# Layer 0 by quarters of the modulation, and later modulation units moved behind queries and values

## The chip, the cores and the metric

The kernel runs on one core of a Trainium2 chip, one launch for the whole model. The metric is the device time of one execution, in microseconds (us); lower is better. TensorE multiplies, VectorE (DVE) and ScalarE (ACT) do elementwise work, GpSimd (POOL) does little here but issue some DMAs, and SyncE (SP) issues nearly all the loads.

## The reference, cut to what matters

The model has two parts of two layers each, on 256 tokens of 1024 features. The change lies in the first part, whose layer is:

```python
c_act = jax.nn.silu(c)
for l in range(DEPTH):                               # DEPTH = 2
    mod = c_act @ w_ada[l] + b_ada[l]                # a vector times 1024 x 6144
    sh1, sc1, g1, sh2, sc2, g2 = jnp.split(mod, 6, axis=-1)
    h = modulate(rmsnorm(x, norm_mix_g[l]), sh1, sc1)   # h * (1 + sc1) + sh1
    proj = h @ w_in[l]                               # conv a, conv gate, q, k, v: 5 x 512 columns
    ...
    y_conv = conformer_conv(u_conv, ...)
    y_att = chunk_band_attention(q, k, v, ..., rel_bias[l])   # 8 heads of 64
    x = x + g1 * (concatenate([y_conv, y_att], -1) @ w_out[l])
    h = modulate(rmsnorm(x, norm_ffn_g[l]), sh2, sc2)
    x = x + g2 * f(h)                                # layer 0 swiglu, layer 1 mixture of experts
```

The six sections of `mod` are numbered 0 to 5 below, in the order sh1, sc1, g1, sh2, sc2, g2.

## The kernel before

Products with weights run in fp32 made of three fp32r products: a 1 MB chunk of weights is loaded (tile `raw`, four buffers for all loads), ScalarE casts its high half and VectorE subtracts to get its low half (`split`, L183 to L188), and `mm3` (L190 to L193) issues high x high, high x low and low x high. A group of 512 output columns (`ca`, `cg` for the conv, `k`, `q`, `v`) is two chunks of four 128-row blocks each, for two tiles of 128 tokens: 48 matmuls of 128x512.

**Modulation.** Sections 0 and 1 of layer 0 are needed first, and are made by quarters of 256 columns (`mod_first`, L402). Of a quarter, section 0 is multiplied on TensorE (L434, the vector's eight pieces as stationary tiles of one column) and section 1 on VectorE (L426, L428). The row of section 0 is copied by ScalarE (L435, `mrow`), then both are turned into columns by tiny matmuls into `mqc` (L447, L448), and ScalarE adds the bias (L449 to L451). `norm_mod` (L455) then scales and shifts the transposed normalized x (`tr`) into the high and low halves `n10h`, `n10l`. The code makes the products of quarter q + 1 in the step of quarter q, and the projections are issued after all quarters.

All other sections are *fillers*, `mod_acc` (L289): a unit loads 1 MB of `w_ada` (two row blocks, `ada` L301) and VectorE adds each block, times its piece of the vector, to an accumulator of 128x1024 (L306, two updates per unit, four units per section). The first unit of a section clears the accumulator on POOL (L297) and loads the section's row of `b_ada` into it (L298). When a section is complete, TensorE sums over partitions, into columns (`mod_cols`, L314, tile `mc`) or rows (`mod_rows`, L326). `mix1` of layer 0 gets the 12 units of sections 2, 3 and 4, and pops one after each chunk of the five projection groups (in `grp`, L503) and one in each of the four attention pairs, with what is left in the last (L751 to L755). Section 5 and the 24 units of layer 1 go to the feed-forward part.

**Attention.** Heads go in four pairs. `bias_of` (L629) loads a pair's relative bias by two DMAs on SP (L637) into one tile and POOL fills two corners (L640, L641). VectorE adds it to the scores `s` and takes maxima (L663, `sbig`), TensorE transposes (`pt`) and multiplies with v (`po`). Convolution products (`cvp`, L617, stationary tiles of 32 columns) run between. At the end come the output projection (chunks `wo040`, `wo041`, `wo000`, `wo001`) and the residual.

A tile framework's scheduler sets the order of instructions on each engine and of the loads from the order of the code, the dependences and the free buffers, so code that stands later may come earlier on an engine that has time by its reckoning.

Of the kernel before, what the change touches and what calls it, by code (L numbers as in the profile page):

```python
# [11 lines left out]
F32 = mybir.dt.float32  # L12
# [5 lines left out]
ALU = mybir.AluOpType  # L18
# [3 lines left out]
P = 128  # L22
# [52 lines left out]
def kernel(ctx: ExitStack, tc: tile.TileContext, I: dict, out: bass.AP, dbg=None, upto=99):  # L75
# [212 lines left out]

    def mod_acc(l, sec, accp):  # L289
# [3 lines left out]
        def unit(k0):  # L293
            def f():
                if k0 == 0:
                    st["acc"] = accp.tile([P, D], F32, tag="acc", name=f"acc{l}{sec}")
                    G.memset(st["acc"], 0.0)  # L297
                    nc.sync.dma_start(st["acc"][0:1, :], I["b_ada"][l : l + 1, sec * D : (sec + 1) * D])  # L298
# [6 lines left out]
                for k in range(2):  # L305
                    V.scalar_tensor_tensor(  # L306
# [8 lines left out]
    def mod_cols(l, which, sec, acc, gain=None):  # L315
# [85 lines left out]

    def mod_first(m, accp):  # L402
# [5 lines left out]

        rows = {}

        def products(q):
            cs = slice(q * 256, (q + 1) * 256)
            raws = []
            for sec in range(2):
# [3 lines left out]
                raws.append(raw.rearrange("p (k c) -> p k c", k=KT))  # L418
            if q == 2:
                ahead["ca0k0"] = load("ca0k0", lambda r: [(  # L420
                    r.rearrange("p (k c) -> p k c", k=4),
                    I["w_in"][0, 0:512, 0:512].rearrange("(k p) c -> p k c", p=P),
                )])
            for k in range(KT):
                if k == 0:
                    V.tensor_scalar(acc[:, cs], raws[1][:, k, :], cact[:, k : k + 1], None, op0=ALU.mult)  # L426
                else:
                    V.scalar_tensor_tensor(  # L428
                        acc[:, cs], raws[1][:, k, :], cact[:, k : k + 1], acc[:, cs], op0=ALU.mult, op1=ALU.add
                    )  # L430
            row = jp.tile([P, 256], F32, tag="tmp", name=f"mrow{q}", bufs=4)
            ps = mmps(f"mq{q}")
            for k in range(KT):
                T.matmul(ps[0:1, :256], cact[:, k : k + 1], raws[0][:, k, :], start=(k == 0), stop=(k == KT - 1))  # L434
            A.copy(row[0:1], ps[0:1, :256])  # L435
            rows[q] = row

        def quarter(q):
            if q == 0:
                products(0)  # L440
            if q < 3:
                products(q + 1)
# [12 lines left out]
    def norm_mod(pool, name, Ac, Bc, before=None):  # L455
# [1556 lines left out]
```

## Time and profile before

| | us |
|---|---|
| median of 3 runs | 2274.03 (2272.07 to 2275.12) |
| the profiled execution | 2275.15 |
| its span | 2273.4 |
| TensorE busy, share of the span | 2199.0, 97% |
| VectorE busy | 1778.3, 78% |
| mean granted TensorE clock, share of 2.4 GHz | .989 |

The times and rows below come from the profiled execution; its time is the span plus 1.7 us around it. A group's busy time adds instructions that overlap at their ends, so the distance between two starts tells what one costs. "Idle before" is the time in which the engine had nothing, and behind the arrow stands what ended it. PEclk is the clock granted to TensorE, as a share of 2.4 GHz, over a stretch, and the lower level is 1.2 GHz.

### The profile page before, as it was taken

To read this page: it belongs to the slowest core of one execution; us is meant where nothing else is said; L and a number is where in the kernel's file an instruction comes from. 1 tells how busy PE (TensorE), PEld (TensorE's weight loads), DVE (VectorE), ACT (ScalarE), POOL (GpSimd) and SP (SyncE) were. 2 spreads that over 40 slices of the span, in tenths; PEclk is the share of its full clock that TensorE was granted. 3 is DMA by queue.
4 is the path that set the end of the run, shared out by engine and by line. 5 is a ranking of instruction groups with operands and counts; after the bars stand their busy time and mean duration, and the time that the engine had idled before them with its cause. 6 is when DMAs were issued, how large, how long until landed. Compare 5 with 4: busy or idle time off the path is not lost. (4 is left out here: it accounts for less than half of the span.)

```text
span 2273.4 us, 29353 instructions
## 1 busy us (share of the span) xinstructions
PE 2199.0 (97%) x10708; PEld 1715.6 (75%) x10708; DVE 1778.3 (78%) x2878; ACT 1411.0 (62%) x2171; POOL 63.1 (3%) x173
## 2 busy tenths in 40 slices
PE   7998998998999999999999999999999999999998
PEld 4766887867878777777778777777777778777776
DVE  7778887657998888889888888987766667766676
ACT  4355334557777777777777777676565556565654
POOL 2300000200000000000000000000000000000000
PEclk9999999999999999999999999999999999999999
DMA  9968796735999999999999999997445445444442
GB/s 328 299 207 279 276 325 226 235 88 200 380 328 352 342 337 359 344 339 332 367 340 350 339 340 361 336 367 227 153 138 177 130 134 171 167 141 131 166 133 85
DMA packets 275758, 587.15 MB, mean 258 GB/s; under 512 B 22796, under 2 KB 42380, under 8 KB 275606
## 3 DMA queue, kind: packets, MB, share of 16 engines
q1 hardware_dynamic: 273302, 580.46, 73.1%
q0 software_dynamic: 2304, 4.74, 0.8%
q8 instruction: 86, 1.41, 0.3%
q14 instruction: 66, 0.54, 0.1%
HBM read 579.80 MB, written 1.05 MB: 255 GB/s over the span
## 5 line engine op out<-in xcount | busy, mean ns | idle before, releaser
L306 DVE SCALAR_TENSOR_TENSOR acc<-ada,cact,acc 128x1024 f32<-128x1024 f32 x80 | 102.3, 1280 | 2.6 <-DMA ada<-in_w_ada_dram 1.5
L491 ACT CAST at<-t 128x512 fp32r<-128x512 f32 x56 | 32.9, 587 | 87.3 <-PE t L1145 87.3
L492 DVE TENSOR_TENSOR at<-t,at 128x512 fp32r<-128x512 f32 x56 | 38.3, 684 | 22.9 <-ACT at L491 22.7
L363 ACT ACTIVATE sqj<-x 128x512 bf16<-128x512 f32 x36 | 22.6, 627 | 45.0 <-DVE x L487 28.4
L1379 ACT ACTIVATE ec<-ec,nmc 128x128 f32<-128x128 f32 x64 | 28.6, 447 | 16.8 <-DVE nmc L1375 16.8
L530 POOL DMA_DIRECT2D zst<-zp x64 | 33.8, 534 | 71.1 <-ACT zp L546 56.8
L617 PE MATMUL cvp<-zst,cw 128*32 128x256 f32 x512 | 33.5, 405 | 0.0
L1731 POOL MEMSET kbd<- 128x64 f32 x2 | 0.3, 152 | 1081.7 <-PE sc L1194 1021.7
L1105 ACT ACTIVATE gh<-g,mcol,mcol 128x256 f32<-128x256 f32 x32 | 18.3, 570 | 18.1 <-PE g L1095 18.1
L617 PEld LDWEIGHTS cvp<-zst,cw 128*32 128x32 f32 x512 | 16.9, 115 | 15.3 <-issue 5.3
L434 PE MATMUL mq<-ada,cact 128*1 128x256 f32 x64 | 17.8, 441 | 10.7 <-DMA ada<-in_w_ada_dram 10.7
L1095 PEld LDWEIGHTS g<-pm,xnt 128*128 128x128 f32 x128 | 20.5, 207 | 4.3 <-issue 2.0
L1095 PE MATMUL g<-pm,xnt 128*128 128x256 f32 x128 | 21.3, 299 | 1.9 <-DVE pm L1087 1.9
L434 PEld LDWEIGHTS mq<-ada,cact 128*1 128x1 f32 x64 | 5.7, 94 | 21.4 <-ACT sqj L363 9.5
L1375 DVE CUSTOM_DVE_ANT_0 ec<-sc,causal 128x128 f32<-128x128 f32 x64 | 19.7, 351 | 2.0 <-PE sc L1390 2.0
L1375 DVE CUSTOM_DVE_ANT_0 ea<-sa,causal 128x128 f32<-128x128 f32 (+1 forms) x32 | 10.2, 353 | 13.9 <-PE sa L1390 13.9
L667 ACT ACTIVATE sbig<-sbig,nm 128x128 f32<-128x128 f32 (+1 forms) x32 | 14.2, 446 | 10.0 <-DVE nm L663 10.0
L1196 DVE TENSOR_TENSOR yacc<-yacc,sc 128x512 f32<-128x512 f32 x28 | 17.9, 682 | 1.1 <-PE sc L1194 0.7
L1379 ACT ACTIVATE eb<-eb,nmb 128x128 f32<-128x128 f32 (+1 forms) x32 | 14.3, 447 | 6.9 <-DVE nmb L1375 6.9
L1106 ACT ACTIVATE xg<-g,mcol,mcol 128x256 fp32r<-128x256 f32 x32 | 18.3, 572 | 0.0
L1403 DVE TENSOR_SCALAR ec<-ec,smc 128x128 f32<-128x128 f32 x64 | 17.2, 316 | 0.6
L486 DVE TENSOR_TENSOR rtmp<-fd,mrow 128x512 f32<-128x512 f32 x12 | 8.1, 687 | 10.9 <-PE fd L193 10.7
(4846 smaller groups left out, 8267.5 us busy)
## 6 DMA issues: line engine op xcount, KB each, us to landing
ada<-in_w_ada_dram SPq DMA_DIRECT2D x48, 1024.0 KB, 6.8
zst<-zp POOLq DMA_DIRECT2D x64, 65.8 KB, 5.9
bias<-in_rel_bias_dram SPq DMA_DIRECT2D x8, 256.0 KB, 5.1
x<-in_x_dram SPq DMA_DIRECT2D x1, 1024.0 KB, 5.2
ca0k0r<-in_w_in_dram SPq DMA_DIRECT2D x1, 1024.0 KB
ca0k4r<-in_w_in_dram SPq DMA_DIRECT2D x1, 1024.0 KB
cg0k0r<-in_w_in_dram SPq DMA_DIRECT2D x1, 1024.0 KB
cg0k4r<-in_w_in_dram SPq DMA_DIRECT2D x1, 1024.0 KB, 5.3
```

The lines of the kernel that those rows point to most:

```text
L306: V.scalar_tensor_tensor(acc, raw[:, k * D : (k + 1) * D], cact[:, k0 + k : k0 + k + 1], acc, op0=ALU.mult, op1=ALU.add)
L363: squares["last"] = A.activation(junk, x[:, t, c * 512 : (c + 1) * 512], AF.Square, accum_out=squares["ss"][:, t, c : c + 1])
L434: T.matmul(ps[0:1, :256], cact[:, k : k + 1], raws[0][:, k, :], start=(k == 0), stop=(k == KT - 1))
L491: A.copy(dst[0][sl], ps)
L492: V.tensor_tensor(dst[1][sl], ps, dst[0][sl].bitcast(F32), op=ALU.subtract)
L530: nc.gpsimd.dma_start(z4[32 * t : 32 * (t + 1), g], zp[32 * g : 32 * (g + 1), i : i + 2, TQ * t : TQ * t + SW])
L617: T.matmul(ps[32 * g : 32 * (g + 1), :S], ws[j // (TQ // 2)][:, g, j % (TQ // 2), :], zst[i][:, g, j : j + S], start=(j == 0), stop=(j == ...
L1095: T.matmul(gp[:, i * S : (i + 1) * S], xn[part][:, t, (k + i) * P : (k + i + 1) * P], pm[:, t].rearrange("p a b -> p (a b)"), start=(n == ...
L1105: A.activation(h[:, i, :], gp[:, i * S : (i + 1) * S], AF.Identity, scale=a_, bias=b_)
L1106: A.activation(xg[0][:, k + i, :], gp[:, i * S : (i + 1) * S], AF.Identity, scale=a_, bias=b_)
L1375: V.tensor_tensor_reduce(out=e[:, SL[t]], in0=ps[:, SL[t]], in1=mask[:, SL[t]], scale=-1.0, scalar=3e38, op0=ALU.add, op1=ALU.min, accum_o ...
L1379: A.activation(e[:, SL[t]], e[:, SL[t]], AF.Exp, bias=nm[:, t : t + 1], scale=-1.0, accum_out=sm[:, t : t + 1])
```

## The change

1. `b_ada` is loaded once and transposed by TensorE into columns (`ball`). Column sections add it when they are finished (one more small VectorE operation); row sections (2 and 5) start their accumulator with a diagonal of it, by one VectorE operation. POOL's clearing and the loads of rows go, and other sections' first update is a plain multiplication.
2. Section 0's product uses a stationary tile of 32 columns (`c32`, one column filled) in four column groups, into a tile of `atps`; ScalarE copies all 128 partitions. The product of a quarter stands directly ahead of its use; the loads of the next quarter stand ahead of it.
3. In layer 0, the weights of ca, cg and k are loaded by quarters of their rows (`first_weights`: `w0a` of 2 x 128 rows for ca and cg, `w0k` of 4 x 128 rows for k), and after each quarter of the norm 36 matmuls use it (`rows_first`).
4. In layer 0, no filler is popped in the projections; three are popped per attention pair.
5. `rel_bias` is loaded from POOL's queue, in both layers.

```diff
+    ball = const.tile([P, 96], F32, name="ball")
+    brow = jp.tile([P, P], F32, tag="tmp", name="brow", bufs=4)
+    nc.sync.dma_start(brow[:96, :], I["b_ada"].rearrange("l (k p) -> (l k) p", p=P))
...
     def mod_acc(l, sec, accp):
...
-                    G.memset(st["acc"], 0.0)
-                    nc.sync.dma_start(st["acc"][0:1, :], I["b_ada"][l : l + 1, sec * D : (sec + 1) * D])
+                    if sec in (2, 5):
+                        V.tensor_tensor(
...
                 for k in range(2):
+                    if k0 + k == 0 and sec not in (2, 5):
+                        V.tensor_scalar(acc, raw[:, 0:D], cact[:, 0:1], None, op0=ALU.mult)
+                        continue
                     V.scalar_tensor_tensor(
...
+            V.scalar_tensor_tensor(r, ps[:, :KT], 1.0, bcols(l, sec), op0=ALU.add, op1=ALU.add)
+            V.tensor_tensor(r, r, gain, op=ALU.mult)
...
     def mod_first(m, accp):
...
+        c32 = accp.tile([P, D], F32, tag="acc", name="c32")[:, : KT * 32].rearrange("p (k c) -> p k c", c=32)
+        G.memset(c32, 0.0)
+        V.tensor_copy(c32[:, :, 0], cact)
...
+        def products(q):
+            cs = slice(q * 256, (q + 1) * 256)
+            ps = atps(f"mq{q}")
+            for k in range(KT):
+                g = k % 4
+                T.matmul(ps[32 * g : 32 * (g + 1), :256], c32[:, k, :], raws[q][0][:, k, :], start=(k < 4), stop=(k >= 4))
...
         def quarter(q):
             if q == 0:
-                products(0)
+                loads_of(0)
             if q < 3:
-                products(q + 1)
+                loads_of(q + 1)
+            products(q)
...
+            if after is not None:
+                after(k // 2, hT)
...
+        def rows_first(q, hT):
...
+            wa = chunk(f"w0a{q}", None, 2048)
+            if q % 2 == 0:
+                ps0["w"] = chunk(f"w0k{q}", None, 2048)
...
+            names = ("ca", "cg", "k")
+            for nm, k in [(nm, k) for k in range(2) for nm in names] if q < 3 else [(nm, k) for nm in names for k in range(2)]:
+                one(nm, k)
...
-                if fillers:
+                if fillers and not before:
                     fillers.pop(0)()
...
-                nc.sync.dma_start(
+                nc.gpsimd.dma_start(
                     bias[:, :, o : o + w], bass.AP(tensor=rb.tensor, offset=base + off, ap=[[1, P], [384, 2], [1, w]])
...
-            if fillers:
-                fillers.pop(0)()
+            for _ in range(3 if before else 1):
+                if fillers:
+                    fillers.pop(0)()
```

The order of the instructions, by engine. **SP's queue**, after the first two quarters' loads. Before (`ada0sq` is quarter q of section s, `ada0s2` and so on the filler units, a name's last number counts up through the program):

```order
L160 DMA ca0k0r_271<-in_w_in_dram 128x4x512
L417 DMA ada003_314<-in_w_ada_dram 128x8x256
L417 DMA ada013_316<-in_w_ada_dram 128x8x256
L298 DMA acc02_421<-in_b_ada_dram 1x1024
L301 DMA ada020_424<-in_w_ada_dram 128x2x1024
L160 DMA ca0k4r_428<-in_w_in_dram 128x4x512
L301 DMA ada022_460<-in_w_ada_dram 128x2x1024
L160 DMA cg0k0r_466<-in_w_in_dram 128x4x512
L301 DMA ada024_498<-in_w_ada_dram 128x2x1024
L160 DMA cg0k4r_502<-in_w_in_dram 128x4x512
L301 DMA ada026_555<-in_w_ada_dram 128x2x1024
```

and after, from the loads of the last quarter:

```order
L458 DMA ada003_408<-in_w_ada_dram 128x8x256
L458 DMA ada013_410<-in_w_ada_dram 128x8x256
L160 DMA w0a3r_412<-in_w_in_dram 128x2x1024
L160 DMA q0k0r_661<-in_w_in_dram 128x4x512
L160 DMA q0k4r_693<-in_w_in_dram 128x4x512
L160 DMA v0k0r_757<-in_w_in_dram 128x4x512
L160 DMA v0k4r_789<-in_w_in_dram 128x4x512
L318 DMA ada020_987<-in_w_ada_dram 128x2x1024
L951 DMA wr_3210<-in_moe_w_router_dram 128x8x8
L953 DMA br_3212<-in_moe_b_router_dram 1x8
L318 DMA ada022_991<-in_w_ada_dram 128x2x1024
L318 DMA ada024_995<-in_w_ada_dram 128x2x1024
```

The weights of all projections now stand ahead of every filler's load, where the two alternated.

**VectorE** ahead of the scores, from the last steps of the root (`rsqk`) to the second half of qT. Before:

```order
L145 SCALAR_TENSOR_TENSOR rsqk0y_784<-rsqk0u_783,rsqk0y_784 128x32
L143 TENSOR_TENSOR rsqk0u_783<-rsqk0y_784 128x32
L144 SCALAR_TENSOR_TENSOR rsqk0u_783<-rsqk0u_783,rsqk0v_781 128x32
L145 SCALAR_TENSOR_TENSOR rsqk0y_784<-rsqk0u_783,rsqk0y_784 128x32
L576 TENSOR_TENSOR k0_674<-k0_674,rsqk0y_784 128x512 x2
L576 TENSOR_TENSOR q0_757<-q0_757,rsqk0y_784 128x512 x2
L306 SCALAR_TENSOR_TENSOR acc04_836<-ada040_839,cact_140,acc04_836 128x1024 x2
L592 TENSOR_SCALAR qT0_882<-tr_889,vec_79 128x4x128
L306 SCALAR_TENSOR_TENSOR acc04_836<-ada042_877,cact_140,acc04_836 128x1024
L592 TENSOR_SCALAR qT0_882<-tr_901,vec_79 128x4x128
```

and after:

```order
L143 TENSOR_TENSOR rsqk0u_736<-rsqk0y_737 128x32
L326 SCALAR_TENSOR_TENSOR acc03_1096<-ada032_1101,cact_146,acc03_1096 128x1024
L144 SCALAR_TENSOR_TENSOR rsqk0u_736<-rsqk0u_736,rsqk0v_734 128x32
L326 SCALAR_TENSOR_TENSOR acc03_1096<-ada032_1101,cact_146,acc03_1096 128x1024
L145 SCALAR_TENSOR_TENSOR rsqk0y_737<-rsqk0u_736,rsqk0y_737 128x32
L326 SCALAR_TENSOR_TENSOR acc03_1096<-ada034_1191,cact_146,acc03_1096 128x1024
L655 TENSOR_TENSOR k0_650<-k0_650,rsqk0y_737 128x512 x2
L655 TENSOR_TENSOR q0_725<-q0_725,rsqk0y_737 128x512 x2
L326 SCALAR_TENSOR_TENSOR acc03_1096<-ada034_1191,cact_146,acc03_1096 128x1024
L671 TENSOR_SCALAR qT0_824<-tr_831,vec_79 128x4x128
L326 SCALAR_TENSOR_TENSOR acc03_1096<-ada036_1195,cact_146,acc03_1096 128x1024
L671 TENSOR_SCALAR qT0_824<-tr_843,vec_79 128x4x128
```

Updates of section 3 (`acc03`) stand where those of section 4 (`acc04`) stood, and more of them between the steps of the root and the scaling of k and q.

**TensorE** at the end of the pairs, about pair 2's output (`po02`), the transposed convolution (`cvT`) and the first output products (`wo`). Before:

```order
L681 MATMUL pt020_1234<-ident_83,sbig0_907 128x128 x3
L681 MATMUL pt021_1240<-ident_83,sbig0_907 128x128 x3
L730 MATMUL cvT00_1256<-ident_83,cv0_1003 128x128 x4
L730 MATMUL cvT01_1265<-ident_83,cv0_1003 128x128 x4
L191 MATMUL wo000_1316<-wo040h_1320,yT00_381 128x512
L192 MATMUL wo000_1316<-wo040l_1321,yT00_381 128x512
L193 MATMUL wo000_1316<-wo040h_1320,yT01_382 128x512
```

and after:

```order
L809 MATMUL cvT01_1270<-ident_83,cv0_945 128x128 x2
L191 MATMUL wo000_1321<-wo040h_1325,yT00_586 128x512
L768 MATMUL po02_1227<-pT020_1219,v0_754 64x256
L768 MATMUL po02_1227<-pT021_1225,v0_754 64x256
L770 MATMUL po02_1227<-pT020_1219,v0_754 64x128
L770 MATMUL po02_1227<-pT021_1225,v0_754 64x128
L191 MATMUL wo001_1322<-wo040h_1325,yT00_586 128x512
L191 MATMUL wo010_1381<-wo041h_1385,yT00_586 128x512
L338 MATMUL mc04_1246<-ones_88,acc04_1210 128x1 x8
L760 MATMUL pt030_1302<-ident_83,sbig0_849 128x128 x3
L191 MATMUL wo011_1382<-wo041h_1385,yT00_586 128x512
L760 MATMUL pt031_1308<-ident_83,sbig0_849 128x128 x3
```

The columns of section 4 (`mc04`) stood ahead of pair 1's transposes, and stand now behind the first three output products, ahead of pair 3's transposes and of the other output products.

## Rows read from the trace of the kernel before

**Rows 1.** Busy us of PE, PEld, DVE, ACT, POOL, PEclk, DMA share, GB/s

```profile
37.60:79.60 42.00, 40.11 (x168) 30.83 (x168) 32.00 (x32) 20.91 (x38) 7.31 (x13) 0.96 0.91 316
91.50:110.00 18.50, 15.58 (x66) 11.89 (x66) 13.30 (x28) 5.56 (x7) 4.76 (x9) 0.91 1.01 319
113.40:145.10 31.70, 28.45 (x347) 16.81 (x347) 22.40 (x59) 21.74 (x60) 2.15 (x7) 0.95 0.92 266
145.10:171.90 26.80, 26.80 (x129) 20.53 (x127) 22.21 (x54) 10.25 (x22) 0.00 (x0) 1.00 0.38 125
...
180.30:360.00 179.70, 178.13 (x806) 142.91 (x807) 152.84 (x154) 75.38 (x94) 4.80 (x5) 0.99 0.87 310
```

**Rows 2.** TensorE's timeline, 22 to 32 us: start, us, instruction [idle before <-releaser]

```profile
22.75 3.61 PE L434 MATMUL mq<-ada,cact 128*1 128x256 f32 x16 [0.59 <-DMA ada<-in_w_ada_dram]
30.90 1.06 PE L283 MATMUL tr<-ident,n10xn 128*128 128x128 f32 x4 [2.72 <-DVE n10h L479]
```

**Rows 3.** ScalarE's timeline, 28 to 33 us

```profile
28.52 0.56 ACT L475 ACTIVATE n10h<-tr,mcol,mcol 128x256 fp32r<-128x256 f32 x1
...
30.14 2.01 ACT L185 CAST ca0k0h<-ca0k0r 128x1024 fp32r<-128x1024 f32 x2
```

**Rows 4.** TensorE's timeline, starts of 128x512 matmuls at two times

```profile
40.05 0.39 PE L192 MATMUL ca0p<-ca0k0l,n10h 128*128 128x512 f32 x1
40.28 0.39 PE L193 MATMUL ca0p<-ca0k0h,n10l 128*128 128x512 f32 x1
...
48.50 0.63 PE L191 MATMUL ca0p<-ca0k4h,n10h 128*128 128x512 f32 x1
48.92 0.63 PE L192 MATMUL ca0p<-ca0k4l,n10h 128*128 128x512 f32 x1
```

**Rows 5.** One stretch behind a gap, columns as in rows 1

```profile
31.90:37.00 5.10, 5.10 (x20) 1.79 (x19) 4.33 (x8) 0.47 (x2) 0.00 (x0) 0.75 1.06 379
```

**Rows 6.** TensorE's timeline, the convolution's products behind the first scores

```profile
114.95 7.12 PE L617 MATMUL cvp<-zst,cw 128*32 128x256 f32 x128
```

**Rows 7.** VectorE's timeline, first quarter of section 1

```profile
13.73 3.61 DVE L428 SCALAR_TENSOR_TENSOR acc<-ada,cact,acc 128x256 f32<-128x256 f32 x7
```

**Rows 8.** VectorE's timeline ahead of the scores and between the pairs

```profile
106.53 0.19 DVE L145 SCALAR_TENSOR_TENSOR rsqk0y<-rsqk0u,rsqk0y 128x32 f32<-128x32 f32 x1
106.76 1.30 DVE L576 TENSOR_TENSOR k<-k,rsqk0y 128x512 f32<-128x512 f32 x2
...
111.69 0.75 DVE L592 TENSOR_SCALAR qT<-tr,vec 128x512 f32<-128x512 f32 x1
...
115.40 0.28 DVE L663 CUSTOM_DVE_ANT_0 sbig<-s,bias 128x128 f32<-128x128 f32 x1
...
116.51 1.28 DVE L306 SCALAR_TENSOR_TENSOR acc<-ada,cact,acc 128x1024 f32<-128x1024 f32 x1
117.71 0.68 DVE L603 TENSOR_TENSOR cw<-ident,w 128x512 f32<-128x512 f32 x1
...
125.69 0.42 DVE L663 CUSTOM_DVE_ANT_0 sbig<-s,bias 128x256 f32<-128x256 f32 x1 [1.32 <-POOL bias L641]
```

**Rows 9.** Groups by line and shape on VectorE: xcount | busy, mean ns

```profile
L186 DVE TENSOR_TENSOR v0k4l<-v0k4r,v0k4h 128x1024 fp32r<-128x1024 f32 x2 | 2.4, 1222 | 2.4 <-ACT v0k4h L185 2.4
```

**Rows 10.** SyncE's queue, the bias load of pair 1

```profile
116.67 0.89 SPq L637 DMA_DIRECT2D bias<-in_rel_bias_dram  x2
```

**Rows 11.** GpSimd's timeline, the second fill of pair 1's bias

```profile
125.24 0.20 POOL L641 MEMSET bias<- 64x128 f32 x1 [2.61 <-DMA bias<-in_rel_bias_dram]
```

**Rows 12.** Loads of tile w in layer 1, issued by GpSimd

```profile
L512 POOL DMA_DIRECT2D w<-in_vec_dram x4: 548/550/558, 388.2 to 389.9; - x4
...
DMA to landing us min/median/max: 4.2/4.7/5.1
```

**Rows 13.** The page's list of DMA issues

```profile
zst<-zp POOLq DMA_DIRECT2D x64, 65.8 KB, 5.9
```

**Rows 14.** VectorE's timeline in layer 1, pair 1

```profile
467.24 0.29 DVE L663 CUSTOM_DVE_ANT_0 sbig<-s,bias 128x128 f32<-128x128 f32 x1 [3.10 <-POOL bias L640]
```

More of the change, by code (lines that the diff above doesn't have):

```diff
@@ L407, in mod_first, with loads_of @@
         acc = accp.tile([P, D], F32, tag="acc", name="acc01")
+        c32 = accp.tile([P, D], F32, tag="acc", name="c32")[:, : KT * 32].rearrange("p (k c) -> p k c", c=32)
+        G.memset(c32, 0.0)
+        V.tensor_copy(c32[:, :, 0], cact)
         rows = {}
-        def products(q):
-            cs = slice(q * 256, (q + 1) * 256)
-            raws = []
+        raws = {}
+        def loads_of(q):
+            raws[q] = []
             for sec in range(2):
@@ L446, in quarter @@
                 g_ = vc("gm0", n, 1)
-                T.matmul(pc_[:, j : j + 1], rows[q][0:1, j * P : (j + 1) * P], ones[0:1, 0:1], start=True, stop=True)
+                T.matmul(pc_[:, j : j + 1], rows[q][:, j * P : (j + 1) * P], ones[:, 0:1], start=True, stop=True)
                 T.matmul(pc_[:, 2 + j : 3 + j], acc[:, n * P : (n + 1) * P], ones[:, 0:1], start=True, stop=True)
@@ L453, in mod_first, with norm_mod @@
         return quarter
-    def norm_mod(pool, name, Ac, Bc, before=None):
+    def norm_mod(pool, name, Ac, Bc, before=None, after=None):
         rstd, sq = rstd_cols(name)
@@ L495, in mix1, with one @@
         w_in = I["w_in"][l]
-        hT = norm_mod(mp, f"n1{l}", m["sc1"], m["sh1"], before=before)
+        ps0 = {}
+        def rows_first(q, hT):
+            if q == 0:
+                ps0.update({nm: [mmps(f"{nm}{l}p{t}") for t in range(2)] for nm in ("ca", "cg", "k")})
+            wa = chunk(f"w0a{q}", None, 2048)
+            if q % 2 == 0:
+                ps0["w"] = chunk(f"w0k{q}", None, 2048)
+            def one(nm, k):
+                kk = 2 * q + k
+                if nm == "k":
+                    (wh, wl), c = ps0["w"], (2 * (q % 2) + k) * 512
+                else:
+                    (wh, wl), c = wa, k * 1024 + 512 * (nm == "cg")
+                for t in range(2):
+                    ts = slice(t * P, (t + 1) * P)
+                    mm3(
+                        ps0[nm][t], hT[0][:, kk, ts], hT[1][:, kk, ts], wh[:, c : c + 512], wl[:, c : c + 512],
+                        kk == 0, kk == KT - 1,
+                    )
+            names = ("ca", "cg", "k")
+            for nm, k in [(nm, k) for k in range(2) for nm in names] if q < 3 else [(nm, k) for nm in names for k in range(2)]:
+                one(nm, k)
+        hT = norm_mod(mp, f"n1{l}", m["sc1"], m["sh1"], before=before, after=rows_first if before else None)
         yT = [mp.tile([P, KT, S], F32R, tag="yT" + "hl"[i], name=f"yT{l}{i}") for i in range(2)]
@@ L548, in gated @@
                 )
-        grp("ca", 0, lambda pss: st.update(a=pss))
-        grp("cg", 512, gated)
+        if before:
+            st["a"] = ps0["ca"]
+            gated(ps0["cg"])
+        else:
+            grp("ca", 0, lambda pss: st.update(a=pss))
+            grp("cg", 512, gated)
         stack(0)
@@ L567, in qk_done @@
             return f
-        grp("k", 1536, qk_done(0, "k"))
+        if before:
+            qk_done(0, "k")(ps0["k"])
+        else:
+            grp("k", 1536, qk_done(0, "k"))
         grp("q", 1024, qk_done(1, "q"))
```

46 lines of the change are left out of this document (31 added, 15 removed).

## The prediction

> **What bounds the kernel now.** I read the busy times by stage first, to find the stages that the change can touch, then TensorE's timeline through them for its gaps and what ends each, then VectorE's timeline at the same places, then the queues. Only the first 180 us of layer 0 get another order over any length; in the feed-forward part behind them TensorE is busy 178.1 of 179.7 us, whatever the loads do.
>
> By stage [rows 1], TensorE is busy 40.1 of 42.0 us while the conv and key projections run (37.6 to 79.6) and 26.8 of 26.8 in the output projection. It has room in the values (15.6 of 18.5), where it waits for weight halves that ACT and VectorE make, and in the attention pairs (28.5 of 31.7). The DMA share is .91 to 1.01 up to 110: loads and TensorE pace this part together. The projections start only at 37.6, since three of the four quarters of the modulation come first. One quarter's chain: its vector product takes 3.61 us and ends at 26.36; the first modulated half starts at 28.52; TensorE goes on at 30.90 after 2.72 idle [rows 2, 3].
>
> **Part 1: quarters.** A quarter's 36 matmuls start 0.23 us from each other at the full clock and 0.42 at the half one [rows 4]: 36 x 0.23 = 8.3 us. Behind the 2.72 us gap the clock was .75 of full from 31.9 to 37.0 [rows 5]; with TensorE's two levels that is half of the 5.1 us at 1.2 GHz, plus the first us from 30.9: 3.6 us at half speed, 1.8 lost. Now a gap stands ahead of every quarter: the product on TensorE, then the steps from 26.36 to the end of the first modulated half at 28.52 + 0.56, 2.7 us, which stay as they are, then one cast of 1.0 us [rows 3], up to 1.5, that ACT does between. The product shrinks: with 32 columns as stationary tile, neighbouring products go to different column groups, as the convolution's do, 128 in 7.12 us = 0.056 each for 128x256 [rows 6], against 3.61 / 16 = 0.23 before. Its eight steps, two passes each, take 16 x 0.056 = 0.9 us; if they did not overlap, 3.6. Idle and product together: 0.9 + 2.7 + 1.25 = 4.9; busy: 8.3 + 1.8 = 10.1. The first product waits for VectorE's first quarter, which ends at 17.3 as before [rows 7], and the 3.4 us of the chain: 20.7. The quarters start at 20.7, 35.7, 50.7, 65.7 and end at 75.8, against 79.6. Were the clock full throughout, they would end at 68.6.
>
> The Trainium skill ("TensorE: Matmul & The Clock Gate", section "HAM oscillation") says that waits between bursts of matmuls put the clock back in each burst. By that every quarter pays as forecast from [rows 5]; without it the quarters would end 7 us earlier, which is the faster rival below.
>
> Queries and values: 4 chunks x 24 matmuls x 0.23 = 22.2 us, without the modulation's matmuls among them: 75.8 + 22.2 = 98.0 (110.0 before). TensorE wins 12 us there.
>
> **Part 2: who is late next.** VectorE. The updates of the modulation are out of the queries and values in the code, yet in VectorE's order 15 of the 24 updates of sections 2 and 3 stand between z and the second qT, ahead of all scores. An instruction holds VectorE for its duration less 0.08, as the next start shows (116.51 + 1.28, then 117.71). So: 15 updates x 1.20 = 18.0; ten 128x512 steps (2 of z, 4 sums of squares, 4 convolution tables) x 0.60 = 6.0; scaling of q and k 2.4; eleven small steps of the root, 0.22 from start to start, 2.4; qT 2 x 0.67 = 1.3 [rows 8]; six halves of weights x (1.22 - 0.08) = 6.8 [rows 9]. Sum 36.9. z starts when the gate is done: the k matmuls (12, 2.8 us) come behind it, and ACT takes 1.3: 75.8 - 2.8 + 1.3 = 74.3. qT is there at 111.2, and VectorE has read pair 0 at 111.2 + 0.5 (scores) + 1.1 (115.40 to 116.51 in [rows 8]) = 112.8, where it was 116.5. Of the 12 us won on TensorE 3.7 are left; it idles some 10 ahead of the scores.
>
> **Part 3: the attention pairs.** One bias tile serves pair after pair, and a load may start only when VectorE has read the one before. Through SP one of them took from 116.67 to its fill at 125.24, 8.6 us [rows 10, 11]; VectorE itself waited 1.32 us for that fill [rows 8], the rest lay under other work, which is now gone from between the pairs. A bias load from POOL is not in the trace. POOL's own loads landed in 4.7 us (issue 0.55 each) and 5.9 [rows 12, 13]. The bounds are 4.7 and 8.6; I take 5.3, between the two of its own queue. Cycle of a pair: 0.55 + 5.3 + 0.5 for the fills + 1.1 = 7.45; pair 3 is read at 112.8 + 3 x 7.45 = 135.2. Ends of the range: -1.8 and +9.9 for the three.
>
> A rule of the Trainium skill speaks against this move ("DMA: Bandwidth & Descriptors", section "Issuing engine by pattern"): plain loads belong on Sync, and its table gives a first byte at about 1 us from GpSimd and 0.6 from Sync. An estimate from that is 3 x 0.4 = 1.2 us for the three pairs; the 4.7 of [rows 12] is below any bias load of layer 0 here, so the trace does not bear it out.
>
> Behind pair 3 VectorE has six updates of section 4 (7.2) and some 1.3 of others: 143.7. Before, these stood ahead of the last pairs. In TensorE's order the columns of section 4 stand ahead of pair 3's transposes and of 92 of the 96 output products, so these start when the last update ends: 16 matmuls of the columns 1.9, output 92 x 0.23 = 21.2, pair 3's transposes and outputs 3, half clock 1.8 again: 27.9. End 171.6, against 171.9 (end of the output stage in [rows 1]): -0.3. With 4.7 us landing it is -2.1, with 8.6 +9.6. What the quarters won is given back by six updates that became late and by biases that nothing covers.
>
> **Part 4: small ones.** Two more updates stand in VectorE's queue in the residual ahead of the feed-forward part: 2 x 1.2, half under TensorE's last products: +1.2 (0 to 2.4). Layer 1's biases go through POOL too; before, pair 1 alone waited, 3.10 us [rows 14]; with one more issue of 0.55: +0.5 (-1 to +3). The memsets and b_ada rows that go ran on POOL and SP beside other work: nothing. The added additions of the columns and the transposition of b_ada lie off the chain, but for section 4's: +0.2.
>
> **Sum.** -0.3 + 1.2 + 0.5 + 0.2 = +1.6 us on the profiled execution of 2275.15 (span 2273.4 and 1.7 around it): 2276.8. That execution lies 1.1 above the median of 2274.03; on the median's scale it is 2275.7, and I write 2276.
>
> **Rivals.** *Faster: the clock stays up.* No 1.8 us is lost in each quarter, the quarters end at 68.6, and VectorE's chain follows z, so all behind it moves by 7: 2269, and with a landing of 4.7 and the residual's updates under cover 2266. For it: the gaps may come out shorter than 4.9. Against: [rows 5], behind a gap of 2.72.
>
> *Slower: POOL's bias loads.* Each takes what the slow one took, 8.6, because 1 MB loads share its engines: three pairs, 3.3 each, +9.9: 2286. It decides from a landing of 6.2 us on, where three times 0.9 reach 2278.6. For it: the modulation's last loads and the output's weights, 1 MB each, now come over these pairs, so the engines are no quieter than at [rows 10]. Against: the 5.9 of [rows 13] is a median taken while the DMA share was 1.01.
>
> *It doesn't do what it says.* The updates stay ahead of the scores; that is in the forecast. If VectorE gets through them under TensorE's work, because loads come earlier, half of the 10 us of idle goes: 2271.
>
> **Chances.** Forecast .50 (its own range 2271 to 2281), faster rival .25, POOL .15, the last .10. A measurement of this kernel can tell 0.2%, 4.5 us, from no change: faster is below 2269.5, slower above 2278.6. Faster: .03 of the forecast, .18 of its rival, .04 of the last: .25. Slower: .11 of the forecast and .14 of POOL: .25. Same .50. The range 2266 to 2284 leaves out the slowest of POOL's case and the best of the faster one.
>
> **What would show it.** The first conv matmuls of the quarters at 20.7, 35.7, 50.7, 65.7, with a granted clock of some .8 between 20 and 76, and eight product steps in 0.9 us. TensorE done with the values near 98, then idle some 10 us with VectorE's qT as the releaser. Pair 0 read near 113, pair 3 near 135, last output product near 172. Part 2 is wrong if the scores start before 108; part 3 if a bias fill comes over 6.5 us behind its issue, or if VectorE never waits for one. The whole is wrong in kind if the feed-forward part or layer 1 differs by more than 3 us.

## The result, and the profile after

The changed kernel is slower: 2291.79 us median of 4 runs (2288.57 to 2292.42) against 2273.09 for the kernel before beside it, a ratio of 1.0078 with a 95% interval of 1.0061 to 1.0096, or 17.8 us. Forecast were 2276 and a range of 2266 to 2284. The profiled execution took 2288.57, with a span of 2286.9 against 2273.4: its rows account for 13.5 of the 17.8, since it is the shortest of its four executions and that of before the longest of its four.

The head of the page after, busy time and share of the span by engine, then the span in 40 slices:

```profile
span 2286.9 us, 29289 instructions
PE 2194.2 (96%) x10709; PEld 1719.6 (75%) x10709; DVE 1778.0 (78%) x2886; ACT 1410.6 (62%) x2172; POOL 66.7 (3%) x180
...
PE   6788999999999999999999999999999999999998
...
DMA  8857887735999999999999999997445345444432
```

TensorE's slices before:

```profile
PE   7998998998999999999999999999999999999998
```

The engines do nearly the same work: TensorE is busy 2194 us against 2199, VectorE 1778 in both. TensorE's waiting grew by 18.3 us (13.5 of span and 4.8 less busy), and its first slices (57 us each) are where that can be. Set side by side, the first gate matmul of the feed-forward part starts at 192.5 where it started at 180.3 (+12.2); the last projection group of layer 1 starts at 456.6 against 444.4 (+12.2); layer 1's last score matmul starts at 497.1 against 483.2 (+13.9). All of it lies in layer 0's mixer, but for 1.7 in layer 1's attention pairs.

**The quarters did better than forecast.** The stretches of the quarters and of the gaps between them, columns as in [rows 1]:

```profile
20.00:30.60 10.60, 10.60 (x40) 8.22 (x40) 8.51 (x14) 4.03 (x6) 0.00 (x0) 1.00 0.94 345
30.60:35.30 4.70, 3.55 (x33) 1.93 (x32) 1.23 (x1) 3.27 (x10) 0.00 (x0) 0.94 0.54 168
35.30:45.20 9.90, 9.90 (x42) 7.71 (x41) 7.26 (x12) 2.80 (x4) 0.00 (x0) 0.86 0.90 330
45.20:50.00 4.80, 3.25 (x27) 1.88 (x26) 2.35 (x2) 3.73 (x10) 0.00 (x0) 1.00 0.65 210
50.00:58.70 8.70, 8.70 (x39) 6.62 (x39) 7.26 (x13) 3.07 (x5) 0.00 (x0) 1.00 0.82 291
58.70:63.50 4.80, 2.79 (x28) 1.80 (x27) 3.55 (x3) 3.69 (x10) 0.00 (x0) 1.00 0.99 323
63.50:71.00 7.50, 7.50 (x32) 6.10 (x33) 2.13 (x5) 2.42 (x6) 0.00 (x0) 1.00 0.92 333
```

The gaps are 4.7 to 4.8 long, and TensorE is busy for 2.8 to 3.6 of each. The third and fourth quarter run at a granted clock of 1.00, the second at .86. Matmuls of the first three quarters, near their starts:

```profile
20.56 0.63 PE L192 MATMUL ca0p<-w0a0l,n10h 128*128 128x512 f32 x1
20.99 0.63 PE L191 MATMUL ca0p<-w0a0h,n10h 128*128 128x512 f32 x1
...
35.91 0.63 PE L192 MATMUL ca0p<-w0a1l,n10h 128*128 128x512 f32 x1
36.34 0.63 PE L191 MATMUL ca0p<-w0a1h,n10h 128*128 128x512 f32 x1
...
50.37 0.39 PE L192 MATMUL ca0p<-w0a2l,n10h 128*128 128x512 f32 x1
50.60 0.39 PE L191 MATMUL ca0p<-w0a2h,n10h 128*128 128x512 f32 x1
```

0.43 from start to start is the lower level of [rows 4], 0.23 the full one. The first quarter starts at the slow spacing too, though the clock recorded over it is 1.00; there the spacing alone shows it. The quarters start at 20.0, 35.3, 50.0 and 63.5, and the last matmul ends at 71.9, 7.7 earlier than before.

**Then the loads stop.** SyncE's queue, the load behind the last weights, a row for layer 1's experts, and the next load:

```profile
63.66 0.37 SPq L318 DMA_DIRECT2D ada<-in_w_ada_dram  x1
...
64.59 1.53 SPq L953 DMA_DIRECT2D br<-in_moe_b_router_dram  x1
76.70 40.36 SPq L318 DMA_DIRECT2D ada<-in_w_ada_dram  x11
```

and the DMA share (second number from the end) behind it, with two later stretches:

```profile
71.00:74.00 3.00, 3.00 (x19) 2.54 (x18) 2.75 (x4) 3.00 (x6) 0.41 (x1) 1.00 0.01 1
74.00:77.00 3.00, 3.00 (x15) 2.43 (x13) 3.00 (x4) 3.00 (x5) 2.68 (x6) 1.00 0.43 93
...
100.00:145.00 45.00, 29.55 (x312) 16.98 (x316) 26.76 (x68) 20.66 (x62) 5.44 (x12) 0.78 0.62 193
```

The queue stands for 10.6 us. From 71 to 74 nothing is loaded (a share of .01), and up to 77 little but the convolution's copies, which GpSimd issues. Where the kernel before alternated weights and filler units, all weights now stand ahead of the units; the four load buffers are full (the second half of q's weights, both of v's, the first unit), and the one that the second unit waits for is freed by the first unit's updates: of the queue's wait, 5.3 us end with the landing of the first unit and 5.2 with VectorE's updates. VectorE's timeline shows where these stand, and what follows up to section 4's last update:

```profile
70.21 1.39 DVE L613 SCALAR_TENSOR_TENSOR z<-th,ca0p 128x512 f32<-128x512 f32 x2 [4.30 <-ACT th L612]
...
75.40 1.28 DVE L326 SCALAR_TENSOR_TENSOR acc<-ada,cact,acc 128x1024 f32<-128x1024 f32 x1
...
83.48 1.28 DVE L326 SCALAR_TENSOR_TENSOR acc<-ada,cact,acc 128x1024 f32<-128x1024 f32 x1 [1.12 <-DMA ada<-in_w_ada_dram]
...
98.53 0.75 DVE L324 TENSOR_SCALAR acc<-ada,cact 128x1024 f32<-128x1024 f32 x1 [6.00 <-DMA ada<-in_w_ada_dram]
...
103.90 1.28 DVE L326 SCALAR_TENSOR_TENSOR acc<-ada,cact,acc 128x1024 f32<-128x1024 f32 x1 [0.63 <-DMA ada<-in_w_ada_dram]
...
113.30 0.75 DVE L671 TENSOR_SCALAR qT<-tr,vec 128x512 f32<-128x512 f32 x1
114.27 0.29 DVE L742 CUSTOM_DVE_ANT_0 sbig<-s,bias 128x128 f32<-128x128 f32 x1 [0.22 <-PE s L729]
...
121.45 0.29 DVE L742 CUSTOM_DVE_ANT_0 sbig<-s,bias 128x128 f32<-128x128 f32 x1 [4.04 <-POOL bias L719]
...
125.65 0.42 DVE L742 CUSTOM_DVE_ANT_0 sbig<-s,bias 128x256 f32<-128x256 f32 x1 [3.61 <-POOL bias L720]
...
143.85 1.28 DVE L326 SCALAR_TENSOR_TENSOR acc<-ada,cact,acc 128x1024 f32<-128x1024 f32 x1
...
152.12 1.28 DVE L326 SCALAR_TENSOR_TENSOR acc<-ada,cact,acc 128x1024 f32<-128x1024 f32 x1
```

The first unit's updates stand behind z; the second ends at 76.68, and at 76.70 the queue goes on. VectorE then waits 1.12, 6.00 and 0.63 for loads, with the steps of the root, k, q and qT queued behind these updates, so TensorE waits 13.29 for k:

```profile
108.58 1.41 PE L283 MATMUL tr<-ident,k 128*128 128x128 f32 x4 [13.29 <-DVE k L655]
...
130.11 1.49 PE L768 MATMUL po<-pT,v 128*64 128x256 f32 x4 [6.23 <-ACT pT L762]
...
131.95 1.65 PE L729 MATMUL s<-kT,qT 64*128 64x128 f32 x6
...
142.37 0.70 PE L729 MATMUL s<-kT,qT 64*128 64x256 f32 x2
...
153.98 0.62 PE L191 MATMUL wo<-wo041h,yT 128*128 128x512 f32 x1 [2.21 <-ACT wo041h L185]
154.39 3.41 PE L338 MATMUL mc<-ones,acc 128*128 128x1 f32 x16
```

In the pairs VectorE waits 7.65 for one bias tile. GpSimd's timeline, the loads (L716, two each) and fills (L719, L720) of pairs 1 to 3:

```profile
116.06 1.43 POOL L716 DMA_DIRECT2D bias<-in_rel_bias_dram  x2 [17.63 <-DVE nm L742]
121.22 0.20 POOL L719 MEMSET bias<- 64x128 f32 x1 [3.73 <-DMA bias<-in_rel_bias_dram]
125.42 0.20 POOL L720 MEMSET bias<- 64x128 f32 x1 [4.00 <-DMA bias<-in_rel_bias_dram]
126.98 1.41 POOL L716 DMA_DIRECT2D bias<-in_rel_bias_dram  x2 [1.36 <-issue]
...
132.12 0.20 POOL L720 MEMSET bias<- 64x128 f32 x1 [1.06 <-DMA bias<-in_rel_bias_dram]
```

From the first issue to the second fill pair 1 takes 9.4, pair 2 5.1 (and pair 3 5.1 again). Beside pair 1 the last unit's 1 MB load was under way (issued by SyncE at 116.7, landed 8.5 later); beside the other two there was none. The pairs are read by 115.5, 126.4, 134.7 and 143.85.

### The profile page after: what moved, and what is told of

The parts are those of the page before. It is cut to its first block, busy times and chain, and to the rows that moved or that the text cites. A ratio compares the mean times of both kernels' runs of the same rounds, so it can differ in the third digit from the quotient of the medians.

```text
span 2286.9 us, 29289 instructions
## 1 busy us (share of the span) xinstructions
PE 2194.2 (96%) x10709; PEld 1719.6 (75%) x10709; DVE 1778.0 (78%) x2886; ACT 1410.6 (62%) x2172; POOL 66.7 (3%) x180
## 5 line engine op out<-in xcount | busy, mean ns | idle before, releaser
L326 DVE SCALAR_TENSOR_TENSOR acc<-ada,cact,acc 128x1024 f32<-128x1024 f32 x74 | 94.7, 1279 | 2.5 <-DMA ada<-in_w_ada_dram 1.8
L602 POOL DMA_DIRECT2D zst<-zp x64 | 34.2, 540 | 96.7 <-ACT zp L618 83.7
L1185 ACT ACTIVATE gh<-g,mcol,mcol 128x256 f32<-128x256 f32 x32 | 18.3, 570 | 17.9 <-PE g L1175 17.9
L1455 DVE CUSTOM_DVE_ANT_0 ea<-sa,causal 128x128 f32<-128x128 f32 (+1 forms) x32 | 10.2, 352 | 13.9 <-PE sa L1470 13.9
L742 DVE CUSTOM_DVE_ANT_0 sbig<-s,bias 128x128 f32<-128x128 f32 (+1 forms) x32 | 10.0, 354 | 13.0 <-POOL bias L719 5.7
L768 PE MATMUL po<-pT,v 128*64 128x256 f32 x32 | 10.1, 498 | 8.6 <-ACT pT L762 8.6
L1186 ACT ACTIVATE xg<-g,mcol,mcol 128x256 fp32r<-128x256 f32 x32 | 18.3, 572 | 0.0
## 6 DMA issues: line engine op xcount, KB each, us to landing
w0a0r<-in_w_in_dram SPq DMA_DIRECT2D x1, 1024.0 KB, 12.5
```

The lines of the kernel that those rows point to most:

```text
L326: V.scalar_tensor_tensor(acc, raw[:, k * D : (k + 1) * D], cact[:, k0 + k : k0 + k + 1], acc, op0=ALU.mult, op1=ALU.add)
L602: nc.gpsimd.dma_start(z4[32 * t : 32 * (t + 1), g], zp[32 * g : 32 * (g + 1), i : i + 2, TQ * t : TQ * t + SW])
L1185: A.activation(h[:, i, :], gp[:, i * S : (i + 1) * S], AF.Identity, scale=a_, bias=b_)
L1186: A.activation(xg[0][:, k + i, :], gp[:, i * S : (i + 1) * S], AF.Identity, scale=a_, bias=b_)
L1455: V.tensor_tensor_reduce(out=e[:, SL[t]], in0=ps[:, SL[t]], in1=mask[:, SL[t]], scale=-1.0, scalar=3e38, op0=ALU.add, op1=ALU.min, accum_o ...
```

## The experiments

All ratios are to the kernel before, run beside each; "us" is (ratio - 1) x 2273. "Units" are the filler units; "as before" means one popped per chunk of a projection group and one per pair. With the quarters kept, only the four chunks of queries and values are left of ten, so there four units leave the pairs and five stand in the last pair; before, ten stood in the projections.

| kernel | what it is | ratio [95%] | us |
|---|---|---|---|
| the change | | 1.0078 [1.0061, 1.0096] | 17.8 |
| e1 | the change, bias on SP | 1.0039 [1.0026, 1.0052] | 8.9 |
| e2 | the change, units as before | 1.0052 [1.0033, 1.0071] | 11.8 |
| e3 | the change, both as before | 1.0026 [1.0015, 1.0038] | 5.9 |
| e4 | before, units in pairs | 1.0044 [1.0028, 1.0060] | 10.0 |
| e5 | before, bias on POOL | 1.0033 [1.0021, 1.0044] | 7.5 |
| e6 | the change, units of half the bytes | 1.0034 [1.0020, 1.0048] | 7.7 |
| e7 | e3, products a quarter ahead | 1.0042 [1.0028, 1.0056] | 9.5 |
| e8 | before, parts 1 and 2 | 1.0017 [1.0007, 1.0026] | 3.9 |
| e9 | the change, two bias tiles | 1.0049 [1.0032, 1.0066] | 11.1 |
| e10 | before, two bias tiles | 1.0006 [0.9997, 1.0016] | 1.4 |
| e12 | e1, units held behind the scores | 1.0038 [1.0024, 1.0053] | 8.6 |
| e13 | e3, a unit in each quarter, `c32` moved | 1.0016 [1.0007, 1.0026] | 3.6 |
| e14 | e3, `c32` moved | 1.0026 [1.0014, 1.0038] | 5.9 |
| e15 | e13, two bias tiles | 1.0012 [1.0001, 1.0022] | 2.7 |
| e16 | e8, `c32` moved | 1.0013 [1.0004, 1.0022] | 3.0 |
| e17 | before, part 1 | 1.0018 [1.0009, 1.0027] | 4.1 |

No version beats the kernel before.

### The queue of the bias loads

Theory A put the loss on the units, B on POOL's bias loads. e1 undoes part 5, e5 makes it alone:

```diff
-                nc.gpsimd.dma_start(
+                nc.sync.dma_start(
```

> The changed kernel with the relative bias loaded from SP's queue again, all else kept. Theory A (the 12 units popped only in the pairs cost the time: updates wait for loads ahead of the scores, six of them and the output weights come late): -3 to +3 us against the changed kernel, 2288 to 2295. Theory B (bias loads from POOL cost it, by some 3 us in each pair of both layers): 8 to 16 us faster than the changed kernel, 2276 to 2284.

> The kernel before with the relative bias loaded from POOL's queue, nothing else. Theory B, as the two runs that put it back on SP measured it (9 us with the units in the pairs, 6 with the units in the projections): 5 to 9 us slower than before, 2278 to 2282. Theory A: within 3 us of before, since there the updates and weights of the output cover the bias.

Measured 2280.85 and 2278.7: 8.9 us less without POOL's loads, 7.5 more with them alone, so B's range is met in both. The pairs of e1 are read by 116.3, 123.3, 130.9 and 139.8: three cycles of 23.5 us together against 28.4, so 4.9 are made in layer 0. e1's loads on SyncE, then its fills on GpSimd:

```profile
116.39 0.88 SPq L716 DMA_DIRECT2D bias<-in_rel_bias_dram  x2
```

```profile
120.43 0.20 POOL L719 MEMSET bias<- 64x128 f32 x1 [22.32 <-DMA bias<-in_rel_bias_dram]
122.32 0.20 POOL L720 MEMSET bias<- 64x128 f32 x1 [1.69 <-DMA bias<-in_rel_bias_dram]
```

5.9 from issue to second fill, and two issues in 0.88 where POOL takes 1.43. Here the last unit's load stands behind the bias loads in the same queue (117.5), where in the change it was issued beside them; pair 2, with no such load, takes 4.6 through SyncE against 5.1 through POOL. So POOL's queue as such is 0.5 slower, and most of pair 1's loss fits the 1 MB load that no longer stands behind. In layer 1 the stretch from the last projection to the last score matmul is 40.5 us in the change, 38.8 before and 36.5 in e1; in e5 it is 38.1, so how much of the cost lies there stays open.

If the one tile makes the wait, a second should hide the load. e9 and e10 give every other pair one of its own:

```diff
+            if a % 2:
+                bias = mp.tile([P, 2, 512], F32, tag="stk", name=f"bias{l}{a}")[:, :, :384]
+            else:
```

> The changed kernel (bias on POOL) with a second bias tile for every other pair, so that a load no longer waits until VectorE has read the pair before. Theory B1 (the load's time stands in the chain of the pairs, once per pair): pairs 0 to 3 are read within 20 us instead of 28.4, and the time falls 6 to 10 us, 2281 to 2286. Theory B2 (POOL's loads are slow for another reason, or disturb others): 3 us at most, 2288 to 2293.

> The kernel before with that second tile, bias on SP. Theory B1: the waits of VectorE for the bias (2.8 and 0.6 us in layer 0, 3.1 in layer 1) go, 2 to 6 us faster than before, 2267 to 2271. Theory B2, or the updates and weights still set the end: within 2 us of before.

It takes 6.6 from the change and nothing from the kernel before. In e9 the pairs are read within 21.8 us (28.4), nearly B1's 20, and all of that is in the first cycle, 3.4 in place of 10.95; pair 0 is read 3.9 later. This fits that in the kernel before work between the pairs covered the wait, and that the change took the cover and lengthened one load.

### Where the units stand

e2 pops the units where they were, e3 has part 5 undone as well, e4 puts part 4 alone on the kernel before:

```diff
-                if fillers and not before:
+                if fillers:
...
-            for _ in range(3 if before else 1):
-                if fillers:
-                    fillers.pop(0)()
+            if fillers:
+                fillers.pop(0)()
```

> The changed kernel with one unit popped after each chunk of queries and values and one per pair, as before; quarters, the bias on POOL and the rest kept. Theory A: 13 to 20 us faster than the changed kernel, 2271 to 2279. Theory B: within 4 us of it, 2288 to 2295.

> The changed kernel with both undone: units popped in queries and values, bias on SP. What is left are the quarters, the 32-column product and the one load of b_ada. Theory A: within 3 us of the run that undoes the units alone. Theory B: 8 us or more below that run. If the quarters win what TensorE shows in the trace (the three projections end at 71.0 instead of 79.6 us), 2264 to 2270; if VectorE and the loads eat it, 2270 to 2275.

> The kernel before with one part of the change alone: no unit popped in the projections of layer 0, three per pair. Theory A: 12 to 20 us slower than before, 2285 to 2293. Theory B: within 3 us of before.

The four units that e2 and e3 take out of the pairs cost 6.0 (the change to e2) and 3.0 (e1 to e3), with intervals that overlap in both; all ten cost 10.0 alone, on a kernel in which nothing else is new. e2 met neither range, e4 fell short of A's 12. What goes out of the early stretch shows in one window of before, of the change and of e3, columns as in [rows 1]:

```profile
20.00:76.00 56.00, 50.45 (x216) 34.99 (x215) 44.07 (x57) 27.38 (x57) 5.71 (x10) 0.94 0.96 335
```

```profile
20.00:76.00 56.00, 51.29 (x250) 38.45 (x251) 37.04 (x53) 28.01 (x56) 2.09 (x4) 0.97 0.79 276
```

```profile
20.00:76.00 56.00, 50.69 (x249) 37.47 (x250) 40.29 (x56) 27.59 (x56) 0.74 (x2) 0.97 0.84 297
```

Up to 76 us VectorE is busy 7 us less in the change than before, and the DMA share falls from .96 to .79. Part of this comes with the quarters, as e3 has it with a share of .84; in e4, by the units alone, VectorE is busy 38.5 us and the share is .93. The units' updates and bytes are not gone, they are made later: from 76 to 116 TensorE is busy 30.7 of 40 us in e4, 35.6 before.

e12 asks whether it is their place ahead of the scores. On e1 it holds each pair's units until its scores are read:

```diff
+            with tc.issue_after(st["read", a].ins) if before else ExitStack():
```

> The changed kernel with the bias on SP and with the three units of each pair held back, by an order on VectorE and nothing else, until that pair's scores have been read: what the change says, done. Against the run with the bias on SP (2280.9): theory A1 (the 15 updates that stand ahead of the scores cost the time, with their loads): scores from 98 to 101 us instead of 113.3, and the time falls 4 to 10 us, 2271 to 2277. Theory A2 (VectorE's total work up to the residual decides, wherever the updates stand): the scores come as early, but the last update and the output end where they did, within 3 us of 2280.9.

The scores came at 97.9 and pair 3 was read by 124.9, 15 us earlier than in e1, and yet the time is that of e1 (1.0038 against 1.0039). The late updates and weights now hold TensorE behind the pairs, as its timeline in e12 shows at a section's columns and at the output's first weights:

```profile
132.52 3.55 PE L338 MATMUL mc<-ones,acc 128*128 128x1 f32 x16 [3.65 <-DVE acc L326]
141.30 0.50 PE L191 MATMUL wo<-wo040h,yT 128*128 128x512 f32 x1 [2.04 <-ACT wo040h L185]
```

So A1's 4 to 10 us did not come. The two intervals still leave a gain or loss of some 4 us, and the profiled execution of e12 (2276.9, below its median of 2279.85) has the first gate matmul at 183.9 against 188.2 in e1's. What is shown is that of 15 us won at the pairs at least ten are lost again behind them; the rows point to what VectorE and the loads still have to do there.

### Loads, and the quarters

e6 tests the loads (theory C) against VectorE's work (D): layer 0's units load one row block and use it twice, so half of sections 2 to 4 is left out, with the same instructions on VectorE.

```diff
+                if l == 0 and sec != 5:
+                    nc.sync.dma_start(raw[:, 0:D], I["w_ada"][l, k0 * P : (k0 + 1) * P, sec * D : (sec + 1) * D])
```

> The changed kernel with half the bytes in each of the 12 units of layer 0 (one row block is loaded and used for both updates, so half of sections 2 to 4 of w_ada is left out), all instructions of VectorE kept. Theory C (the loads ahead of the scores pace them, as 7.8 us of VectorE's waits for ada tell): pair 0 read at 107 to 110 us instead of 115.4, the time 5 to 9 us below the changed kernel, 2281 to 2287. Theory D (VectorE's own work and order pace them): within 2 us of it.

It takes 10.1 from the change, more than C expected. VectorE no longer waits for `ada` between z and the scores, and from z to the reading of pair 0 it takes 37.6 us in place of 45.3: 7.6 less, where the three waits were 7.75. Pair 0 is read by 107.5 in place of 115.5, and the first gate matmul starts at 183.5 in place of 192.5: of these 9.0 us, 8.0 are there by pair 0.

e7 makes e3's products a quarter ahead, as the kernel before does; e14 moves `c32` from the accumulators' pool to a scratch tile:

```diff
             if q == 0:
+                products(0)
...
-            products(q)
+                products(q + 1)
```

```diff
-        c32 = accp.tile([P, D], F32, tag="acc", name="c32")
+        c32 = jp.tile([P, KT * 32], F32, tag="tmp", name="c32", bufs=4)
```

> The kernel with units in the projections and the bias on SP (quarters kept), and the products of quarter q + 1 made a quarter ahead again, so their two buffers come free earlier. Theory C: loads run on in the quarters, the DMA share up to 80 us rises from .86 to over .93, and the time falls 3 to 6 us, 2274 to 2278. Theory D: within 2 us of 2280.6, or slower, since the products push back the halves.

> Quarters kept, bias on SP, one unit per chunk of queries and values and per pair, and the 32-column tile in a scratch tile; it differs from the run before only in that no unit stands in the quarters. Theory E: within 3 us of 2280.6, since the units still start behind the quarters. If the held accumulator alone were the cause, it would fall to 2275 or below.

Neither helps, as D and E had it. In e7 the DMA share up to 80 us is .82, not over .93; the first quarter waits for the second one's load and starts at 27.2, the scores at 120.5.

e13 gives the early stretch back its updates: e14 with one unit popped in each quarter. e15 has two bias tiles as well.

```diff
+            if fillers:
+                fillers.pop(0)()
```

> Quarters kept, bias on SP, and the units spread: one behind each quarter, one behind each chunk of queries and values, one per pair. For that the 32-column tile stands in a small scratch tile instead of the second accumulator, which it held until the last quarter's product. Theory E (VectorE and the loads had room in the quarters and the change took the units away from there): VectorE busy over 42 of the 56 us from 20 to 76 as before (37.2 in the run with bias on SP), the time 5 to 12 us under the run with units in the projections and the bias on SP (2280.6), 2268 to 2275. Rival F (four load buffers: units in the quarters push back the quarters' own loads): the quarters end at 76 or later and the time is 2276 to 2283.

> The kernel with units in the quarters, and a second bias tile. Theory B1: VectorE's remaining waits for the bias go; 1 to 4 us below the same kernel with one tile, 2265 to 2273 under theory E; within 2 us of it if, as in the kernel before, other work sets the pairs.

2277.16 and 2276.17, 2 to 3 us below e3 with intervals that overlap, not the gain expected; e15's second tile adds as little. The stretch 20 to 76 has VectorE busy 38.8 us in e13, at a DMA share of .82; e14, without the units there, has 34.2 and .84, e3 40.3. The 42 that theory E asked for did not come about, so E's gain is not shown and its room not refuted. Rival F is what happened: with four units among them the first quarter starts at 25.5, and the queries behind the last at 82.0, later than the 79.6 of before. In these runs the quarters win time on TensorE only as long as the loads of the units stand back.

### Parts 1 and 2 alone

What e3 leaves is 5.9. e8 has `b_ada` loaded once and the product by 32 columns alone (no quarters of weights, no other order of the products), e16 the same with `c32` moved, e17 `b_ada` alone (the first hunk of the diff ahead of the prediction, with `mod_acc` and the columns).

> The kernel before with two parts of the change alone: b_ada loaded once, and section 0's product by a stationary tile of 32 columns in four column groups. Neither the quarters of the weights, nor the units, nor the bias are moved. TensorE's products shrink from 3.6 to 1.1 us, four of them, of which two wait for loads in any case: 0 to 5 us faster than before, 2268 to 2273, if the start of the projections moves; the same if the loads pace it.

> Parts 1 and 2 alone, as in the experiment with the bias rows and the column product alone, but with the 32-column vector in a scratch tile and no longer in the accumulators' pool. Theory G (the vector's tile held the second accumulator, so that the first filler started only when the quarters were done and the loads stopped between 30 and 50 us): the DMA share of 40 to 50 us rises from .43 to .75 or more, the scores start before 117 in place of 120.6, and the time is 2268 to 2274. Theory H (the loads stop for another reason, or what they lose does not count): the scores stay within 2 us of 120.6 and the time within 2 us of 2276.2.

> Part 1 alone: b_ada loaded once and transposed, no clearing and no row loads of the accumulators; everything else as before. Theory G (what parts 1 and 2 cost together lies in the column product and its tile): within 2 us of the kernel before, 2271 to 2275. Rival I (the extra work on VectorE and the transposition ahead of the first product cost it): 2275 to 2279.

The three agree, at 3.9, 3.0 and 4.1: the column product and its tile cost nothing that can be seen here (theory G fell; in e16 the share of 40 to 50 us is .38), and part 1, which had been priced at 0.2, costs some 4. Rival I's range holds, but not the place that it gave: in e17 the first conv matmul starts at 35.9, earlier than the 37.6 of before. VectorE's timeline in e17 between the last half of v's weights and the second qT:

```profile
106.30 1.28 DVE L326 SCALAR_TENSOR_TENSOR acc<-ada,cact,acc 128x1024 f32<-128x1024 f32 x1
...
108.30 1.22 DVE L310 TENSOR_TENSOR acc<-ident,ball 128x1024 f32<-128x1024 f32 x1
...
110.85 1.28 DVE L326 SCALAR_TENSOR_TENSOR acc<-ada,cact,acc 128x1024 f32<-128x1024 f32 x1
...
117.61 0.75 DVE L613 TENSOR_SCALAR qT<-tr,vec 128x512 f32<-128x512 f32 x1
```

Seven steps of 1.2 us (one start of an accumulator, six updates) stand between 104 and the second qT, where there were three before. The code pops the units at the same places; with part 1 the scheduler's order has them earlier, ahead of the scaling of k and q, and the second qT starts at 117.6 in place of 113.6. In the profiled execution only 1.7 of these are left at the feed-forward part, and its whole span, 2271.7, is 1.7 shorter than that of before. The 4.1 are of the ratio; that this order makes them is argued, not shown.

## Why the prediction was wrong, step by step

**What bounds the kernel.** The feed-forward part passed the 12.2 us on unchanged, as said. But the stretch ahead of it was read as paced by "loads and TensorE together", and the sum then followed TensorE and VectorE alone.

**Part 1: right in kind, too careful.** The gaps were forecast at 4.9 and are 4.7 to 4.8, the product at 0.9 and is 1.07. Matmuls at the slow spacing cost the first two quarters 2.3 and 1.5, not 1.8 in each, and the others lost 0.4 and 0.2. The Trainium skill's rule weighed there ("TensorE: Matmul & The Clock Gate", section "HAM oscillation"), that waits between bursts of matmuls put the clock back in each burst, is borne out by the second quarter and not by the last two, whose gaps are as long. TensorE was busy for 2.8 to 3.6 us of each gap, so these were not bare waits. The faster rival was half right, 71.9 against its 68.6 and the 75.8 of the sum, and the time did not fall with it.

**Part 2: the step that failed first.** The chain on VectorE from z to qT was put at 36.9 us of work, with the updates' data taken to be there. The work was right: z at 70.2, the end of the second qT at 114.0, 43.8 less 7.75 of waits is 36.0. The missing term is the loads: the order of SyncE's queue, all weights ahead of all units, was printed ahead of the prediction, and was not followed to the point where four buffers are full and the queue stands for 10.6 us. e6 shows that term: with half of the bytes the waits are gone. Pair 0 was read at 115.5, 2.7 later than forecast: z came 4.1 earlier, the waits added 7.75, the work was 0.9 less. (Sections 2 and 3 have 16 updates; the 24 named there are those of sections 2 to 4. The 15 is right.)

**Part 3: the term that was mis-sized.** Three cycles of 7.45 were forecast; they took 10.95, 8.3 and 9.2, 28.4 in all, 6.0 more. The first, 3.5 over, is the bias load, 9.4 us from issue to second fill where 5.85 were forecast. This is the POOL rival's mechanism and more than its price (8.6), for one pair of three: pairs 2 and 3 took 5.1, less than forecast. It was given little for the 5.9 of [rows 13], the time of another, smaller load under other conditions; over the whole kernel e1 and e5 measure 8.9 and 7.5 for the bias on POOL, near the rival's 9.9, so its chance of .15 was too small. The other two cycles are 0.8 and 1.7 over for a term that the cycle left out, TensorE's own work in the pairs: pair 2's scores stand behind pair 1's output on TensorE, which waited 6.23 for it, and pair 3's last scores start at 142.37, behind pair 2's output. e1 and e9 take 9.0 and 8.9 for that third cycle as well. The Trainium skill's rule on plain loads ("DMA: Bandwidth & Descriptors", section "Issuing engine by pattern") pointed the right way. The 1.2 us estimated from its figures for three pairs were far too few: e1's three cycles are 4.9 shorter.

**Behind the pairs.** The six updates took 9.6 (forecast 8.5), and the last output product started 30.1 behind them (27.9): the output's weights were loaded from 141 on, and TensorE waited 2.21 for a half of them. The residual, forecast at +1.2, cost 0.5. Layer 1's biases cost 1.7 (0.5).

Together, over the forecast: 2.7 + 6.0 + 1.1 + 2.2 - 0.7 + 1.2 = 12.5, with the 1.6 of the forecast 14.1 where the span shows 13.5.

**"Nothing" for the small ones.** Part 1's clearing and row loads that go were costed by their own work, at nothing. e17 measured 4.1. Its rows show another order of the updates, the likely cause; that stays open.

**What stays open.** The parts alone (4.1, 10.0 and 7.5 for parts 1, 4 and 5) add to 21.6 before the quarters; the whole is 17.8. Whether the quarters give back 4 beside the others, or cost 2 as e3 against e8 has it, the intervals don't tell.

## What to carry to other kernels

An operation that leaves a stretch where its engine had room doesn't leave the program: list what the stretch loses in updates and in bytes, and find where they are made up before anything won on the pacing engine is counted. When the order of loads changes, walk the queue with the number of buffers in hand, and ask which instruction frees the buffer that the next load waits for and where that one stands. A load with one buffer between two uses must be priced with the loads that run beside it, once the work that covered it is moved: here 9.4 us beside a 1 MB load of another queue, 5.1 without one.

## What the runs showed of the hardware

Two small loads issued by GpSimd occupied it 1.43 us, and 0.88 on SyncE; issued by GpSimd beside a 1 MB load, the second was usable 9.4 us after the first issue, and 5.1 without one (4.6 on SyncE in e1). Gaps of 4.8 us with TensorE busy 2.8 to 3.3 in them had a granted clock of 1.00 behind them, one of 4.7 with 3.55 busy had .86; what made the difference no run here shows.
